# Seven products instead of eight in more of the gate and up columns, and a norm's sum two steps later

## The chip, the cores and the metric

The kernel is one program on one core of a Trainium2 chip. TensorE (PE in the profile) does the matrix products, VectorE (DVE) and ScalarE (ACT) the elementwise work, GpSimd (POOL) a little of it, and SyncE (SP) issues most of the DMAs. The metric is the device time of one execution in microseconds (us), the median of several runs.

## The reference

One layer on 256 rows of width 2048, in float32:

```python
x = x + 0.5 * swiglu(rms_norm(x, ffn1_norm), w_gate, w_up, w_down)     # FFN 1
u, q, k, v = split(rms_norm(x, mix_norm) @ w_in)
y_ssm = glu(s5(u))                                                      # state-space heads
y_sb = stick_breaking_attention(rms_norm(q), rms_norm(k), v)
x = x + concat(rms_norm(y_ssm), rms_norm(y_sb)) @ w_out
x = x + 0.5 * swiglu(rms_norm(x, ffn2_norm), w_gate, w_up, w_down)      # FFN 2
x = x + rms_norm((p @ w_ple_proj) * sigmoid(rms_norm(x, ple_norm) @ w_ple_gate))

def swiglu(h, w_gate, w_up, w_down):
    return (silu(h @ w_gate) * (h @ w_up)) @ w_down
```

The gate and up weights are 2048 x 5632, the down weights 5632 x 2048. All weights of the two FFNs are read once.

## The kernel before

**The float32 product.** Each float32 operand is split into a high part (a cast, on ScalarE) and a low part (what the cast left, a subtraction on VectorE). A product is then three matmuls of 128x128 by 128x512: high by high (L305), low activation by high weight (L306), high activation by low weight (L310). Weights arrive in a `raw` tile of four k tiles (128 rows of k each) by 512 columns, 1 MB, in a ring of five. `split` (L178) makes of each half of it, two k tiles, a tile `whi` (L181) and a tile `wlo` (L184), in rings of four. The 256 rows are two row tiles, so a half costs 2 x 2 x 3 = 12 matmuls. After each half `step()` advances the generators that run beside (transposes, norms, and in FFN 1 the preparation of the state-space part). `put_off(n, f)` runs `f` after `n` such steps.

**Gate and up.** Each FFN has 11 blocks of 512 columns, f = 0 to 10. A plain block runs all k (16 k tiles, eight halves) for the gate and then for the up columns: 16 halves. In FFN 1 (i=1, `bg` is the preparation) all blocks are plain. In FFN 2 block 0 is plain, and blocks 1 to 10 use the class `Seven`.

**Seven.** For a quarter of k, gate and up together, two row tiles and two halves of k make 2x2 by 2x2 blocks, so eight products of six matmuls each. `chunk(kb)` does quarter kb with seven products instead (Winograd's form of Strassen's method): 42 matmuls instead of 48. Three of the products use weights as they are. Four use sums of weights: VectorE adds them (`add`, L487, ring `sum` of two), ScalarE casts the sum to `shi`, and VectorE subtracts for `slo` (rings of three). These are called own products below, with their low parts `slo`. Against them stand `sum_forms` of the activations, made once per quarter of k from `whole_rows` (L426) with four additions (L441) and a split. `column(side, kbs)` does the quarters that are left over in the plain way, side 0 the gate and side 1 the up columns. The banks are combined afterwards: `opened` adds products 1, 6 and 7 (L574 to L576), `gated` products 2, 4 and 5 (L580 to L583), and L593 and L595 finish the block. Before, a block of FFN 2 is one chunk (quarter 0), then three quarters of the gate, then three of the up columns. The down projections of both FFNs use `Seven` too, by plans of their own.

**Order.** A scheduler chooses the order of the instructions on each engine within the data's dependences and the rings. Only pinned instructions keep their written place. Each engine then runs its own list in order.

**The norm in the middle.** `glu` writes the state-space output; its squares are added up on GpSimd (`add_square`, L1304 on ScalarE and L1305 on GpSimd), and `rms(steps, ...)` sums them over rows with two small matmuls against ones (L1289, pinned), `steps` steps later, and takes the inverse root (`rsqrt_mean`, L198 to L209, with a table load before ScalarE's square root at L203). The first user of the result is L1438, which takes the output projection's banks to x.

Of the kernel before, what the change touches and what calls it, by code (L numbers as in the profile page):

```python
# [33 lines left out]
def layer_kernel(ctx: ExitStack, tc: tile.TileContext, a: dict, shapes: dict, out: bass.AP):  # L34
# [3 lines left out]
    SW = shapes["ssm_d"][1]  # L38
# [34 lines left out]
    def phase(name):  # L73
        return tc.tile_pool(name=name, bufs=1, reuse_waits="tile")
# [354 lines left out]
        )  # L429
        return u.rearrange("p j n -> p (j n)").rearrange("p (j x b) -> p j x b", j=4, b=32)  # L430

    def sum_forms(pool, u):

        sums = pool.tile([P, 2, NB], F32, tag="sum", name=uid("rows"), bufs=2)
        s = sums.rearrange("p j n -> p (j n)").rearrange("p (z j x b) -> p z j x b", z=4, j=2, b=32)
        (a11, a21), (a12, a22) = ([u[:, k : k + 2, 4 * t : 4 * t + 4] for t in range(TT)] for k in (0, 2))
        for z, (x, y, op) in enumerate((
            (a21, a22, ALU.subtract), (s[:, 0], a11, ALU.subtract),
            (a11, a21, ALU.subtract), (a12, s[:, 1], ALU.add),
        )):  # L440
            nc.vector.tensor_tensor(out=s[:, z], in0=x, in1=y, op=op)  # L441
        both = halves("n")
        split(*both, sums.rearrange("p j n -> p (j n)").rearrange("p (z t) -> p z t", z=4))
        return both

# [93 lines left out]
    def ffn(i, xn, nxt, bg=None):  # L539
        wg, wu, wd = (a[f"ffn{i}_w_{s}"][0] for s in ("gate", "up", "down"))  # L540
        hT = []
        pools = ExitStack()
        early = 8 if bg else NF
        sevens = None if bg else pools.enter_context(phase(f"sums{i}"))
        hp = pools.enter_context(phase(f"h{i}"))
        side = ExitStack()
# [14 lines left out]
                hT.append(by_tile(hf, n_pair))  # L561

        for f in range(NF):
            if prep and f == min(early, NF - 1):
                finish(prep)
                side.close()
                prep = None
                hp = pools.enter_context(phase(f"h{i}b"))
            if sevens and f:
                sg, hh = com("sg"), com("h")  # L570
                gate_cols, up_cols = ([u[:, t * NB : (t + 1) * NB] for t in range(TT)] for u in (sg, hh))

                def opened(s, g=gate_cols, u=up_cols):
                    nc.scalar.copy(g[0], s.bank(1))  # L574
                    nc.vector.tensor_tensor(out=u[0], in0=s.bank(6), in1=g[0], op=ALU.add)
                    nc.vector.tensor_tensor(out=u[1], in0=s.bank(7), in1=u[0], op=ALU.add)  # L576

                def gated(s, g=gate_cols, u=up_cols, hh=hh):
                    for z, (ps, other) in enumerate(((s.bank(2), g[0]), (s.bank(4), u[1]))):
                        nc.vector.tensor_tensor(out=g[z], in0=ps, in1=other, op=ALU.add)  # L580
                        nc.scalar.activation(g[z], g[z], AF.Silu, scale=xn.rs(z))
                    v = hh.rearrange("p (t n) -> p t n", t=TT)
                    nc.vector.tensor_tensor(  # L583
                        out=v, in0=s.bank(5).unsqueeze(1).to_broadcast([P, TT, NB]), in1=v, op=ALU.subtract
                    )

                s = Seven(xn, lambda kb: sums[kb], ((wg, f * NB), (wu, f * NB)), sevens)
                s.chunk(0, shared)
                put_off(0, opened, s)
                s.column(0, (1, 2, 3), True)  # L590
                put_off(0, gated, s)
                s.column(1, (1, 2, 3), True)
                nc.vector.tensor_tensor(out=hh, in0=s.banks[3.8], in1=hh, op=ALU.add)  # L593
                for t in range(TT):
                    nc.vector.scalar_tensor_tensor(  # L595
                        out=up_cols[t], in0=up_cols[t], scalar=xn.rs(t), in1=gate_cols[t], op0=ALU.mult, op1=ALU.mult
                    )
                put_off(2, turned, hp, f, hh)
                continue

            def gate():
                for t in range(TT):
                    nc.scalar.activation(sg[:, t * NB : (t + 1) * NB], pg[t], AF.Silu, scale=xn.rs(t))

            first = ()
            if f == 0 and bg:
                warm_up(10)
                first = first_quarters(wg, xn)
            if f == 0 and not bg:
                both = gemm_pair(xn, ((wg, 0), (wu, 0)), KD)  # L610
                pg = next(both)
                sums = [sum_forms(sevens, whole_rows(sevens, xn(0)))]
            else:
                pg = gemm_block(xn, wg, f * NB, KD, first)
            sg = com("sg")
            if f == 0 and bg:
                for n in range(ND):
                    put_off(n, load_x, n)
                    put_off(n + 2, xn.squares, n)
                put_off(6, gate)  # L620
            else:
                gate()
            pu = gemm_block(xn, wu, f * NB, KD) if f or bg else next(both)
            if prep and f == 0:
                start(prep)
            hh = com("h")
            for t in range(TT):
                nc.vector.scalar_tensor_tensor(
                    out=hh[:, t * NB : (t + 1) * NB], in0=pu[t], scalar=xn.rs(t),
                    in1=sg[:, t * NB : (t + 1) * NB], op0=ALU.mult, op1=ALU.mult,  # L630
                )
            put_off(2, turned, hp, f, hh)
# [6 lines left out]
        def act(k):  # L639
            hi, lo = halves("h")  # L640
            split(in_32(hi), in_32(lo), rows(k))
            return hi, lo

        if not sevens:
            sevens = pools.enter_context(phase(f"sums{i}"))

        def gather(x, ps, scale):
            nc.vector.scalar_tensor_tensor(out=x, in0=ps, scalar=scale, in1=x, op0=ALU.mult, op1=ALU.add)
# [692 lines left out]
    def glu(pool, zs):  # L1341

        w = a["ssm_w_glu"][0]
        sq_acc = get(pool, "sqg", T)
        parts = []
        for n in range(SW // NB):
            ps = [acc(), acc()]
            for k0 in range(0, SW // P, 4):
                zhi, zlo = zs[k0 // 4]
                for h, hi, lo in weight_halves(w, k0, 4, n * NB):  # L1350
                    for part in range(2):
                        for j in range(2):
                            kt = k0 + 2 * h + j
                            for c in range(4):
                                o = ps[c // 2][:, (c % 2) * T : (c % 2 + 1) * T]
                                cs = slice(c * P, (c + 1) * P)
                                zj = 2 * h + j
                                if part == 0:
                                    nc.tensor.matmul(
                                        o, lhsT=hi[:, j, cs], rhs=zhi[:, zj, :], start=kt == 0 and c % 2 == 0,  # L1360
                                        stop=False, skip_group_check=True,
                                    )
                                    nc.tensor.matmul(
                                        o, lhsT=hi[:, j, cs], rhs=zlo[:, zj, :], start=False, stop=False,
                                        skip_group_check=True,
                                    )
                                else:
                                    nc.tensor.matmul(
                                        o, lhsT=lo[:, j, cs], rhs=zhi[:, zj, :], start=False,
                                        stop=kt == SW // P - 1, skip_group_check=True,  # L1370
                                    )
                    step()
            sg, y = com("sg"), com("h")
            hi, lo = halves("n")
            for c in range(4):
                nc.scalar.activation(
                    sg[:, c * T : (c + 1) * T], ps[c // 2][:, (c % 2) * T : (c % 2 + 1) * T], AF.Sigmoid,
                    bias=col("ssm_b_glu", 4 * n + c),
                )
            for t in range(TT):  # L1380

                su = sg.rearrange("p (c s t k) -> p c s t k", c=4, s=SL, t=TT)[:, :, :, t, :]
                zu = zt[0][:, :, 4 * n : 4 * n + 4, t * NC // TT : (t + 1) * NC // TT].rearrange("p s c k -> p c s k")
                yu = y.rearrange("p (c t s k) -> p c s t k", c=4, s=SL, t=TT)[:, :, :, t, :]
                nc.vector.tensor_tensor(out=yu, in0=su, in1=zu, op=ALU.mult)
            split_each(
                hi, lo, y.rearrange("p (c t) -> p c t", t=T), [col("out_norm_ssm", 4 * n + c) for c in range(4)]
            )
            for c in range(4):
                add_square(pool, sq_acc, y[:, c * T : (c + 1) * T], 4 * n + c == 0)  # L1390
            parts.append((hi, lo))
        return parts, rms(3, sq_acc, SW)


    n1, nm, n2, npl = Normed("ffn1_norm", load_turned), Normed("mix_norm"), Normed("ffn2_norm", kinds="hhnn", late=0), Normed("ple_norm", late=0)
# [256 lines left out]
```

## Time and profile before

| | |
|---|---|
| median of 3 runs | 1859.77 us (1859.67 to 1860.08) |
| the profiled execution | 1859.97 us, its span 1858.1 us |
| PE, PEld, DVE, ACT, POOL busy | 1848.8, 1530.4, 1350.9, 991.8, 62.8 us |
| matmuls recorded | 9098 |
| granted TensorE clock | 1.00 |

A row of the timeline or of the groups names the line, the engine, the operation, the tile written and the tiles read; "idle before" is the time in which the engine stood still before it, with what it then waited for. PEld is the load of weights into TensorE, which runs beside the matmuls.

### The profile page before, as it was taken

How to read it: one execution, taken by the hardware profiler on the slowest of the kernel's cores; microseconds unless marked ns; L12 is line 12 of the kernel's file. 1: busy time of each engine (PE TensorE's matmuls, PEld its weight loads, DVE VectorE, ACT ScalarE, POOL GpSimd, SP SyncE). 2: the span in 40 equal slices, each digit the busy share in tenths (PEclk: the TensorE clock that was granted, in tenths of full speed). 3: DMA queues.
4: the chain of work that ended last, by engine and by line, in shares of the span. 5: the costliest groups of instructions: out<-in, count | busy, mean ns of one | idle time of the engine just before them, and what ended most of it. 6: DMA issues, size and time to landing. Idle time of an engine off the chain costs nothing.

```text
span 1858.1 us, 23916 instructions
## 1 busy us (share of the span) xinstructions
PE 1848.8 (100%) x9098; PEld 1530.4 (82%) x9098; DVE 1350.9 (73%) x1599; ACT 991.8 (53%) x1147; POOL 62.8 (3%) x108
## 2 busy tenths in 40 slices
PE   9999999999999999999999999999999999999998
PEld 7888888888888888888888888888888888888887
DVE  8967764555688976687567677878788868897755
ACT  7444444444455656456695555555554545565654
POOL 0011000000000000010021000000000000000000
PEclk9999999999999999999999999999999999999999
DMA  9888868676656667675646776576666675666663
GB/s 330 283 278 269 256 218 231 201 230 200 217 188 219 200 208 255 183 260 166 218 153 201 236 266 216 192 226 204 221 210 206 195 244 183 212 198 225 200 226 125
DMA packets 232307, 406.37 MB, mean 219 GB/s; under 512 B 26784, under 2 KB 50720, under 8 KB 231904
## 3 DMA queue, kind: packets, MB, share of 16 engines
q1 hardware_dynamic: 227824, 392.81, 64.6%
q0 software_dynamic: 3648, 10.62, 1.8%
q8 instruction: 71, 1.16, 0.3%
q10 hardware_dynamic: 720, 1.41, 0.2%
q14 instruction: 44, 0.36, 0.1%
HBM read 373.46 MB, written 11.93 MB: 207 GB/s over the span
## 4 chain that ended last, share of the span: by engine, by line
PE 96%; ACT 2%; DVE 1%; DMA 0%; POOL 0%; issue 0%; SPq 0%; DVEq 0%; POOLq 0%
PE acc L305 22%; PE acc L310 22%; PE acc L306 22%; PE aux L306 7%; PE aux L305 7%; PE aux L310 7%; PE acc L480 2%; PE acc L481 2%; PE acc L483 2%; PE aux L480 1%; PE aux L481 1%; PE aux L483 1%; PE aux L1114 0%; ACT whi L181 0%; DMA raw<-in_ffn_w_gate 0%; ACT nhi L191 0%
## 5 line engine op out<-in xcount | busy, mean ns | idle before, releaser
L184 DVE TENSOR_TENSOR wlo<-raw,whi 128x1024 fp32r<-128x1024 f32 x650 | 789.0, 1223 | 412.3 <-ACT whi L181 398.7
L181 ACT CAST whi<-raw 128x1024 fp32r<-128x1024 f32 x650 | 680.9, 1053 | 761.6 <-PE acc L306 497.9
L305 PE MATMUL acc<-whi,nhi 128*128 128x512 f32 x1408 | 550.8, 391 | 1.3 <-ACT whi L273 0.8
L306 PE MATMUL acc<-whi,nlo 128*128 128x512 f32 x1408 | 548.3, 389 | 0.0
L310 PE MATMUL acc<-wlo,nhi 128*128 128x512 f32 x1408 | 384.4, 389 | 0.1
L305 PEld LDWEIGHTS acc<-whi,nhi 128*128 128x128 f32 x1408 | 264.3, 188 | 58.2 <-ACT whi L273 1.9
L310 PEld LDWEIGHTS acc<-wlo,nhi 128*128 128x128 f32 x1408 | 264.2, 188 | 55.6 <-DVE wlo L184 0.6
L306 PEld LDWEIGHTS acc<-whi,nlo 128*128 128x128 f32 x1408 | 264.3, 188 | 54.2 <-DVE nlo L274 0.3
L305 PE MATMUL acc<-whi,hhi 128*128 128x512 f32 x416 | 161.8, 389 | 0.0
L306 PE MATMUL acc<-whi,hlo 128*128 128x512 f32 x416 | 161.8, 389 | 0.0
L305 PE MATMUL aux<-whi,hhi 128*128 128x512 f32 x384 | 149.4, 389 | 0.0
L306 PE MATMUL aux<-whi,hlo 128*128 128x512 f32 x384 | 149.4, 389 | 0.0
L310 PE MATMUL acc<-wlo,hhi 128*128 128x512 f32 x416 | 126.7, 389 | 0.0
L310 PE MATMUL aux<-wlo,hhi 128*128 128x512 f32 x384 | 118.2, 389 | 0.0
L306 PEld LDWEIGHTS acc<-whi,hlo 128*128 128x128 f32 x416 | 78.1, 188 | 16.2
L305 PEld LDWEIGHTS acc<-whi,hhi 128*128 128x128 f32 x416 | 78.1, 188 | 16.2
L310 PEld LDWEIGHTS acc<-wlo,hhi 128*128 128x128 f32 x416 | 78.1, 188 | 16.2
L310 PEld LDWEIGHTS aux<-wlo,hhi 128*128 128x128 f32 x384 | 72.1, 188 | 15.0
L305 PEld LDWEIGHTS aux<-whi,hhi 128*128 128x128 f32 x384 | 72.1, 188 | 15.0
L306 PEld LDWEIGHTS aux<-whi,hlo 128*128 128x128 f32 x384 | 72.1, 188 | 15.0
L184 DVE TENSOR_TENSOR slo<-sum,shi 128x1024 fp32r<-128x1024 f32 x64 | 77.9, 1218 | 0.0
L181 ACT CAST shi<-sum 128x1024 fp32r<-128x1024 f32 x64 | 67.4, 1053 | 16.3 <-DVE sum L487 13.2
(324 smaller groups left out, 1739.6 us busy)
## 6 DMA issues: line engine op xcount, KB each, us to landing
raw<-in_ffn_w_up SPq DMA_DIRECT2D x88, 1024.0 KB, 5.7
raw<-in_ffn_w_down SPq DMA_DIRECT2D x88, 1024.0 KB, 5.1
raw<-in_ffn_w_gate SPq DMA_DIRECT2D x86, 1024.0 KB, 5.8
raw<-in_w_in SPq DMA_DIRECT2D x32, 1024.0 KB, 5.8
raw<-in_w_out SPq DMA_DIRECT2D x16, 1024.0 KB, 5.3
raw<-in_w_ple_gate SPq DMA_DIRECT2D x16, 1024.0 KB, 5.5
hT<-mid SPq DMA_DIRECT2D x160, 64.0 KB, 2.7
h<-mid SPq DMA_DIRECT2D x176, 32.0 KB, 3.8
```

Of the source, the lines that this page charges most:

```text
L181: copy = nc.scalar.copy(hi, src)
L184: nc.vector.tensor_tensor(out=lo, in0=src, in1=hi.bitcast(F32), op=ALU.subtract)
L305: nc.tensor.matmul(ps[t], lhsT=lh, rhs=hi[:, j, cols], start=start and j == 0, stop=False)
L306: nc.tensor.matmul(ps[t], lhsT=ll, rhs=hi[:, j, cols], start=False, stop=False)
L310: nc.tensor.matmul(ps[t], lhsT=lh, rhs=lo[:, j, cols], start=False, stop=stop and j == 1)
L480: nc.tensor.matmul(ps, lhsT=lh[j], rhs=hi[:, j], start=begin and j == 0, stop=False)
L481: nc.tensor.matmul(ps, lhsT=ll[j], rhs=hi[:, j], start=False, stop=False)
L483: nc.tensor.matmul(ps, lhsT=lh[j], rhs=lo[:, j], start=False, stop=z in final and j == 1)
```

## The change

There are four edits.

1. FFN 2: every odd block (1, 3, 5, 7, 9) does two quarters of k as chunks: chunk 0, the gate's quarters 2 and 3, chunk 1, the up columns' quarters 2 and 3. The combining (`opened`, then `gated`) follows chunk 1. The sum forms of quarter 1 are made as well.
2. FFN 1: blocks 7 to 10 use `Seven`. Block 7 does the gate's quarters 1 to 3 first, then chunk 0, then the up columns' quarters 1 to 3. Blocks 8 and 10 have two chunks, block 9 has one.
3. For that, the sum forms of quarters 0 and 1 are made at block 7 of FFN 1, and the preparation that runs beside FFN 1 is finished there (`finish(prep)`) instead of at block 8.
4. The sum of squares of the state-space output is taken five steps later instead of three.

```diff
-        early = 8 if bg else NF
+        early = 7 if bg else 0
...
-            if prep and f == min(early, NF - 1):
+            if prep and f == early:
                 finish(prep)
                 side.close()
                 prep = None
+                sevens = pools.enter_context(phase(f"sums{i}"))
                 hp = pools.enter_context(phase(f"h{i}b"))
+                sums = [sum_forms(sevens, whole_rows(sevens, xn(kb)), "h") for kb in range(2)]
...
-                s.chunk(0, shared)
-                put_off(0, opened, s)
-                s.column(0, (1, 2, 3), True)
+                two = f % 2 == (0 if bg else 1)
+                if f == early:
+                    s.column(0, (1, 2, 3))
+                    s.chunk(0, (*shared, 2, 4))
+                    put_off(0, opened, s)
+                elif two:
+                    s.chunk(0)
+                    s.column(0, (2, 3))
+                    s.chunk(1, (*shared, 2, 4))
+                    put_off(0, opened, s)
+                else:
+                    s.chunk(0, shared)
+                    put_off(0, opened, s)
+                    s.column(0, (1, 2, 3), True)
                 put_off(0, gated, s)
-                s.column(1, (1, 2, 3), True)
+                s.column(1, (2, 3) if two and f != early else (1, 2, 3), True)
...
-                sums = [sum_forms(sevens, whole_rows(sevens, xn(0)))]
+                sums = [sum_forms(sevens, whole_rows(sevens, xn(kb))) for kb in range(2)]
...
-        return parts, rms(3, sq_acc, SW)
+        return parts, rms(5, sq_acc, SW)
```

The new lines shift the numbers: L574 to L583 become L576 to L585, L593 and L595 become L606 and L608, L628 becomes L641, and L979 and everything behind it is ten higher (L1304 is L1314, for example). L184, L441 and L487 stay.

The first place is VectorE at block 7 of FFN 1. Before, these rows are the low parts of plain halves only (in a plain block there are 16 of them):

```order
L184 TENSOR_TENSOR wlo_2912<-raw_2909,whi_2911 128x1024
L184 TENSOR_TENSOR wlo_2916<-raw_2909,whi_2915 128x1024
L184 TENSOR_TENSOR wlo_2951<-raw_2948,whi_2950 128x1024
L184 TENSOR_TENSOR wlo_2955<-raw_2948,whi_2954 128x1024
L184 TENSOR_TENSOR wlo_2989<-raw_2986,whi_2988 128x1024
```

In the changed kernel the second sum form (`rows`, `hlo`) and the chunk's sums and own low parts stand between them:

```order
L441 TENSOR_TENSOR rows_2832<-whole_2830,rows_2832 128x256
L184 TENSOR_TENSOR wlo_2955<-raw_2950,whi_2954 128x1024
L487 TENSOR_TENSOR sum_2965<-raw_2950,raw_2952 128x1024
L184 TENSOR_TENSOR hlo_2838<-rows_2832,hhi_2837 128x1024
L184 TENSOR_TENSOR wlo_3016<-raw_2950,whi_3015 128x1024
L184 TENSOR_TENSOR slo_2968<-sum_2965,shi_2967 128x1024
L487 TENSOR_TENSOR sum_2978<-sum_2965,raw_2952 128x1024
L184 TENSOR_TENSOR wlo_3026<-raw_2952,whi_3025 128x1024
L487 TENSOR_TENSOR sum_2991<-sum_2978,raw_2950 128x1024
L184 TENSOR_TENSOR slo_2981<-sum_2978,shi_2980 128x1024
L184 TENSOR_TENSOR wlo_3039<-raw_3036,whi_3038 128x1024
L184 TENSOR_TENSOR slo_2994<-sum_2991,shi_2993 128x1024
```

Between two plain low parts there are now additions and the low parts of sums, and wlo_3039, of the up columns, comes ahead of the chunk's last low parts.

The second place is VectorE in FFN 2 where the next chunk's sums begin. Before, the first sums (L487) come late in a single block, among plain low parts:

```order
L184 TENSOR_TENSOR wlo_9999<-raw_9992,whi_9998 128x1024
L487 TENSOR_TENSOR sum_10119<-raw_10104,raw_10106 128x1024
L487 TENSOR_TENSOR sum_10132<-sum_10119,raw_10106 128x1024
L580 TENSOR_TENSOR sg_9794<-acc_9866,sg_9794 128x512
L184 TENSOR_TENSOR wlo_10034<-raw_10031,whi_10033 128x1024
L580 TENSOR_TENSOR sg_9794<-acc_9843,h_9795 128x512
L184 TENSOR_TENSOR slo_10122<-sum_10119,shi_10121 128x1024
L583 TENSOR_TENSOR h_9795<-acc_9817,h_9795 128x1024
```

In the changed kernel, at the end of a double block, they come right behind the last own low part of that block's chunk 1 (slo_10175), with all of the combining behind them:

```order
L184 TENSOR_TENSOR slo_10175<-sum_10172,shi_10174 128x1024
L487 TENSOR_TENSOR sum_10300<-raw_10285,raw_10287 128x1024
L487 TENSOR_TENSOR sum_10313<-sum_10300,raw_10287 128x1024
L577 TENSOR_TENSOR h_9962<-aux_9997,sg_9961 128x512
L184 TENSOR_TENSOR slo_10303<-sum_10300,shi_10302 128x1024
L578 TENSOR_TENSOR h_9962<-aux_9997,h_9962 128x512
L582 TENSOR_TENSOR sg_9961<-acc_10033,sg_9961 128x512
L582 TENSOR_TENSOR sg_9961<-acc_10010,h_9962 128x512
L184 TENSOR_TENSOR wlo_10249<-raw_10246,whi_10248 128x1024
L585 TENSOR_TENSOR h_9962<-acc_9984,h_9962 128x1024
```

The five combining steps that a block had spread over its columns stand together at the boundary of two chunks.

The third place is ScalarE around the norm's square root. Before, the table load and the root (L203) stand ahead of the last four squares (L1304), which come some rows later:

```order
L181 COPY whi_8207<-raw_8201 128x1024
L203 ACT_TABLE_LOAD
L203 ACTIVATE sm_8146<-sm_8144 128x2
L181 COPY whi_8263<-raw_8261 128x1024
L191 ACTIVATE nhi_8223<-aux_8178,gains 128x256 x4
L181 COPY whi_8267<-raw_8261 128x1024
```

In the changed kernel the four squares (now L1314) come first:

```order
L191 ACTIVATE nhi_8365<-aux_8305,gains 128x256 x4
L181 COPY whi_8409<-raw_8403 128x1024
L1314 ACTIVATE sqp_8375<-aux_8305 128x256
L1314 ACTIVATE sqp_8378<-aux_8305 128x256
L1314 ACTIVATE sqp_8381<-aux_8305 128x256
L1314 ACTIVATE sqp_8384<-aux_8305 128x256
L203 ACT_TABLE_LOAD
L203 ACTIVATE sm_8333<-sm_8331 128x2
```

The root, and with it L1448 (L1438 before), now stands behind the four squares. On PE the two pinned matmuls (L1289, now L1299) move behind two more halves and the attention output's small matmuls.

On SP the rest of the preparation's DMAs (eight writes of scr_h, eight reads m, one write of scr_m) was spread among six loads of weights. In the changed kernel only two loads stand among them.

More of the change, by code (lines that the diff above doesn't have):

```diff
@@ L430, in whole_rows, with sum_forms @@
         return u.rearrange("p j n -> p (j n)").rearrange("p (j x b) -> p j x b", j=4, b=32)
-    def sum_forms(pool, u):
+    def sum_forms(pool, u, kind="n"):
         sums = pool.tile([P, 2, NB], F32, tag="sum", name=uid("rows"), bufs=2)
@@ L441, in sum_forms @@
             nc.vector.tensor_tensor(out=s[:, z], in0=x, in1=y, op=op)
-        both = halves("n")
+        both = halves(kind)
         split(*both, sums.rearrange("p j n -> p (j n)").rearrange("p (z t) -> p z t", z=4))
@@ L642, in act @@
             return hi, lo
-        if not sevens:
-            sevens = pools.enter_context(phase(f"sums{i}"))
         def gather(x, ps, scale):
```

## The prediction

> **What bounds the kernel now.** I read the page first: busy times, then the chain of work that ended last.
>
> ```profile
> PE 1848.8 (100%) x9098; PEld 1530.4 (82%) x9098; DVE 1350.9 (73%) x1599; ACT 991.8 (53%) x1147; POOL 62.8 (3%) x108
> PEclk9999999999999999999999999999999999999999
> PE 96%; ACT 2%; DVE 1%; DMA 0%; POOL 0%; issue 0%; SPq 0%; DVEq 0%; POOLq 0%
> ```
>
> TensorE is busy for 1848.8 of the span's 1858.1 us at the full granted clock, and the chain is TensorE's for 96%. VectorE is at 73% on average. What does TensorE wait for? The waits of PE:
>
> ```profile
> PE aux L1289 <- POOL sqg L1305: 1.8, 1, 1.8
> PE aux L248 <- POOL ones L125: 1.1, 1, 1.1
> PE acc L305 <- ACT whi L273: 0.8, 1, 0.8
> PE acc L305 <- ACT whi L181: 0.4, 1, 0.4
> ```
>
> That is 4.1 us in all, 1.8 of it at the norm that edit 4 touches. So a matmul less is its time less, as long as the other engines keep up. Averages don't tell that, so I took the busy times of the engines over single blocks: one plain block of FFN 1 (about block 8), and two neighbours in FFN 2, each with one chunk. The columns are PE, PEld, DVE, ACT and POOL busy (with counts), the clock, the DMA share and GB/s.
>
> ```profile
> 359.60:403.10 43.50, 43.50 (x194) 36.02 (x193) 23.06 (x21) 18.03 (x19) 0.00 (x0) 1.00 0.69 216
> 1134.00:1176.30 42.30, 42.30 (x188) 34.93 (x187) 33.10 (x32) 21.57 (x23) 0.00 (x0) 1.00 0.70 222
> 1176.30:1218.60 42.30, 42.30 (x188) 34.93 (x187) 35.22 (x35) 21.66 (x23) 0.00 (x0) 1.00 0.62 201
> ```
>
> A chunk brings TensorE from 43.5 to 42.3 us and VectorE from 23.1 to some 34.2 us (the mean of the two), with the combining in it. TensorE waits for nothing in either.
>
> **What a chunk saves.** The timeline of PE, the first matmul of a chunk (L480), and the first behind it (L305):
>
> ```profile
> 1176.49 0.39 PE L480 MATMUL acc<-whi,hhi 128*128 128x512 f32 x1
> ...
> 1186.13 0.39 PE L305 MATMUL acc<-whi,hhi 128*128 128x512 f32 x1
> ```
>
> The chunk's 42 matmuls take 1186.13 − 1176.49 = 9.64 us, 0.2295 each. A plain block of 16 halves, 192 matmuls, in 43.5 us gives 0.2266 each. The quarter pair that a chunk replaces has 48, so 10.88 us. Saved: 1.24 us a chunk, and the two windows agree (43.5 − 42.3 = 1.2). The change adds five chunks in FFN 2 and six in FFN 1 (1 + 2 + 1 + 2), 66 matmuls less: 11 × 1.24 = **13.6 us**. Casts cost nothing: ScalarE is busy for half of each window, and a double block adds it three more casts.
>
> **What it adds on VectorE.** Four sums and three low parts a chunk. Their price is not their duration but the distance of their starts, which the timeline of DVE shows ahead of a chunk:
>
> ```profile
> 1166.16 1.22 DVE L487 TENSOR_TENSOR sum<-sum,raw 128x1024 f32<-128x1024 f32 x1
> 1167.31 1.22 DVE L184 TENSOR_TENSOR wlo<-raw,whi 128x1024 fp32r<-128x1024 f32 x1
> 1168.44 1.22 DVE L184 TENSOR_TENSOR slo<-sum,shi 128x1024 fp32r<-128x1024 f32 x1
> 1169.58 1.22 DVE L184 TENSOR_TENSOR wlo<-raw,whi 128x1024 fp32r<-128x1024 f32 x1
> ...
> 1181.12 1.22 DVE L184 TENSOR_TENSOR slo<-sum,shi 128x1024 fp32r<-128x1024 f32 x1
> ...
> 1189.73 1.23 DVE L184 TENSOR_TENSOR wlo<-raw,whi 128x1024 fp32r<-128x1024 f32 x1 [1.48 <-ACT whi L181]
> ```
>
> Starts are 1.13 to 1.15 apart, 1.135 on average, although each lasts 1.22. So a second chunk costs 7 × 1.135 = 7.9 us, and a double block needs 34.2 + 7.9 = 42.1 us of VectorE against 43.5 − 2 × 1.24 = 41.0 of TensorE. Alone it would be too much, but in FFN 2 a single block follows: 76.3 against 83.3 us a pair. The slack is there as gaps of 1.48 us between the column's low parts (last row).
>
> The Trainium skill speaks against this price: its page "VectorE: DVE Perf Modes", section "The DRAIN you can't avoid", says that the next operation does not start until the pipe has emptied. With a full 1.22 us for each of the some 32 large operations of a double block, it would need 2.7 us more, 44.8 against 41.0; the rows above, 1.135 apart, do not show such a hold, and the section itself adds that an operation that is not held starts earlier.
>
> **FFN 2's boundaries.** The last own low part of the chunk above starts at 1181.12 and is done at 1182.34. TensorE wants it behind five products, near 1182.7: a margin of 0.4 us, here at the end of a single block. At a double block's end the combining (two additions of 0.68 and 0.69, two of 0.69, one of 1.22) stands at the same place:
>
> ```profile
> 1184.58 0.68 DVE L575 TENSOR_TENSOR h<-aux,sg 128x512 f32<-128x512 f32 x1
> 1185.29 0.69 DVE L576 TENSOR_TENSOR h<-aux,h 128x512 f32<-128x512 f32 x1
> L580 DVE TENSOR_TENSOR sg<-acc,h 128x512 f32<-128x512 f32 x10 | 6.9, 688 | 1.3 <-PE acc L310 1.3
> L583 DVE TENSOR_TENSOR h<-acc,h 128x1024 f32<-128x1024 f32 x10 | 12.2, 1218 | 0.0
> ```
>
> Counting the changed order off from the end of chunk 1 at these distances, VectorE runs without a gap to the next chunk's last low part, and comes just in time: 0 to 0.5 us each. There are four such boundaries to a next chunk and one to the down projection. I take **0.8 us** in all, from 0 (the margin) to 5 (1 us each, one operation too many). Chunk 1 inside a double block has some 5 us of lead.
>
> **FFN 1, blocks 7 to 10.** Here VectorE gets six chunks in four blocks, and two sum forms of an addition (1.135), four quarter additions and a low part (1.135). The quarter rows:
>
> ```profile
> L441 DVE TENSOR_TENSOR rows<-hT 128x256 f32<-128x256 f32 x12 | 4.5, 419 | 0.0
> ...
> 316.41 1.41 DVE L628 SCALAR_TENSOR_TENSOR h<-acc,sm,sg 128x512 f32<-128x512 f32 x2 [1.09 <-PE acc L310]
> ...
> 318.87 1.30 DVE L216 STREAM_TRANSPOSE mid<-h 128x512 f32<-128x512 f32 x2
> ```
>
> At some 0.36 apart (an estimate between the 0.42 they last and the overlap seen above) that is 3.7 a form, 7.4 for both. The sum is 2 × 34.2 + 2 × 42.1 + 7.4 = 160.0 us of VectorE in 4 × 43.5 − 6 × 1.24 = 166.6 of TensorE, 96% full. Such a stretch can't be free of waits, since the work comes in heaps. In block 7 the changed order has, from L628 at 316.41 to the chunk's last own low part, 22 large operations (25.0 us), eight quarter rows (2.9) and L628 and L216 (2.7): ready at 347.0. TensorE begins block 7 at 316.15 and reaches that low part behind 131 matmuls (29.7), at 345.85: 1.2 us late. The same count gives 1.3 at block 8's first chunk, next to nothing at its second, 1.3 at block 9's. I take **4.0 us**; from 1 (the scheduler's interleaving of column halves covers it) to 8 (each chunk late by 1.3).
>
> **The norm.** TensorE's wait of 1.77 us at L1289 goes, since GpSimd is done two halves earlier than it is asked:
>
> ```profile
> 968.53 0.71 PE L1289 MATMUL aux<-ones,sqg 128*128 128x128 f32 x4 [1.77 <-POOL sqg L1305]
> 963.57 4.91 POOL L1305 TENSOR_TENSOR sqg<-sqg,sqp 128x256 f32<-128x256 f32 x4 [11.90 <-ACT sqp L1304]
> 969.13 1.28 ACT L203 ACT_TABLE_LOAD   x1
> 971.84 0.59 PE L1313 MATMUL aux<-w,v 128*128 128x256 f32 x2
> ...
> 974.23 0.38 PE L1317 MATMUL aux<-w,v 128*128 128x128 f32 x2
> 977.44 1.40 DVE L1438 SCALAR_TENSOR_TENSOR x<-acc,sm,x 128x512 f32<-128x512 f32 x2
> 982.22 0.38 ACT L1304 ACTIVATE sqp<-aux 128x256 f32<-128x256 f32 x1 [1.34 <-POOL sqa L1305]
> ```
>
> What is late next: the root stands behind four squares, two of which wait for GpSimd's additions of about 1.2 us each. TensorE would come to the two matmuls at 968.53 − 1.77 = 966.76, plus 5.44 for two halves and 2.7 for the attention's small matmuls (971.84 to 974.6), which now stand ahead of them: 974.9. Counted on from there, the squares end near 978.6, the table load near 979.9, and L1448 hands back its banks near 982 and 982.6, while TensorE is through its pair of columns near 980.8. It waits some 1.3 us there for a bank. Gain 1.77 − 1.3, about **0.4 us**, between +1.8 (no such wait) and −1.5 (the squares' second half late by one addition for each of them).
>
> **The sum.** Against the profiled 1859.97 us (1858.1 of span, 1.87 around it; 0.20 above the median): 13.6 + 0.4 − 4.0 − 0.8 = 9.2 us less. From the median, 1859.8 − 9.2 = **1850.6 us**.
>
> **Rivals.** A: no wait at all is left, the matmul count decides alone: 1859.8 − 13.6 − 0.4 = 1845.8. For it: before, 10 chunks of FFN 2 run without a wait. Against: there VectorE has gaps ahead of every chunk, and 4% slack is far less.
>
> B, slower: VectorE falls behind for good in blocks 7 to 10. A chunk's own product is a chain of sum (1.22), ScalarE's cast and subtraction (1.22), and a row gives the cast:
>
> ```profile
> L181 ACT CAST whi<-raw 128x1024 fp32r<-128x1024 f32 x650 | 680.9, 1053 | 761.6 <-PE acc L306 497.9
> ```
>
> So 1.22 + 1.05 + 1.22 = 3.5 us. If each of the six chunks bares one such chain, 21 us go: 1859.8 − 13.6 − 0.4 + 21 + 0.8 = 1867.6. It decides from 14.0 us of waits on, 1.27 for each added chunk. For it: 96%. Against: three slots for own parts let the chains overlap. Were the 114 large operations of these blocks 1.22 apart and not 1.135, VectorE would need 9.7 us more, 169.7 against 166.6. That is what the Trainium skill's rule weighed above would make of them.
>
> C: the drained preparation blocks SP. Before, its DMAs were spread out:
>
> ```profile
> 291.29 2.49 SPq L979 DMA_DIRECT2D scr_h<-hq  x4
> ...
> 307.73 2.18 SPq L986 DMA_DIRECT2D m<-scr_h  x4
> ...
> 324.06 0.37 SPq L990 DMA_DIRECT2D scr_m<-m  x1
> scr_h<-hq SPq DMA_DIRECT2D x8, 32.0 KB, 5.1
> m<-scr_h SPq DMA_DIRECT2D x2, 128.0 KB, 6.4
> ```
>
> In one go, eight writes (2 × 2.49), a landing (5.1), eight reads (2 × 2.18) and their landing (6.4) are 21 us, with one load of weights let through; TensorE eats one every 5.44 us (half a quarter pair), and five slots hold 27 us. It fits by a few us. If not, loads for block 7 are late by about one landing more, 5 us: 1855.7.
>
> **Chances.** Forecast 0.65, A 0.15, B 0.12, C 0.08. The range has to leave out no more than 0.2: from A, 1845.5, up to 1857.0, where FFN 1 loses 8, the boundaries 3 and the norm gains nothing (2.6 us gained). A measurement can tell 0.2%, 3.7 us, from no change: below 1856.1 is faster. Faster: nearly all of the forecast, A, half of C, 0.81. Within: the rest of these and a corner of B, 0.09. Slower: 0.10, B.
>
> **What would show it.** PE's busy time down by 13 to 14 us and L305's groups with fewer matmuls; new waits of PE for `slo` or `whi` (L184, L181) between 330 and 470 us, a few of about 1 us each; blocks 8 and 10 of FFN 1 near 41 to 43 us; double blocks of FFN 2 near 41.0 and the singles behind them 42.3 to 42.8; the row PE aux L1289 gone, and one wait of 1 to 1.5 us for L1448 near 980. I am wrong if the waits in FFN 1 pass 8 us, if a wait at every boundary of FFN 2 passes 1 us, or if DMA stands as the releaser of block 7's casts.

## The result, and the profile after

The changed kernel takes 1851.99 us (1851.55 to 1852.70, five runs), the kernel before 1859.88 (1859.67 to 1860.13): 7.9 us less, a ratio of 0.9958 [0.9944, 0.9973]. The forecast was 1850.6 us, 9.2 less.

The busy times and the chain on the page of the changed kernel:

```profile
span 1850.6 us, 23946 instructions
PE 1838.3 (99%) x9032; PEld 1518.5 (82%) x9032; DVE 1460.6 (79%) x1718; ACT 1027.4 (56%) x1187; POOL 63.3 (3%) x108
PEclk9999999999999999999999999999999999999999
PE 92%; DVE 3%; DMA 2%; ACT 2%; SPq 1%; issue 1%; DVEq 0%; ACTq 0%
```

The 66 matmuls are gone (9098 to 9032), VectorE has 110 us more to do, and the chain is no longer TensorE's alone. What TensorE waits for, in the waits of PE:

```profile
PE acc L480 <- ACT shi L181: 2.6, 2, 1.7
PE acc L305 <- ACT whi L181: 1.7, 3, 1.1
PE aux L248 <- POOL ones L125: 1.1, 1, 1.1
PE aux L480 <- ACT shi L181: 0.9, 1, 0.9
PE acc L310 <- DVE wlo L184: 0.3, 2, 0.2
```

The first and fourth rows are new: L480 is a chunk's matmul, `shi` the cast of a sum. So is the 1.1 us in the second row, which stands at the norm; the section on why the prediction was right comes back to it. The wait for GpSimd at the norm is gone. Where the time went is read from the same matmul in both timelines of PE: the first of FFN 1's down projection, of FFN 2's gate, of FFN 2's down projection, and the last. Before:

```profile
490.51 0.39 PE L305 MATMUL acc<-whi,hhi 128*128 128x512 f32 x1
1048.41 0.39 PE L305 MATMUL acc<-whi,hhi 128*128 128x512 f32 x1
1514.73 0.39 PE L305 MATMUL acc<-whi,hhi 128*128 128x512 f32 x1
1852.05 1.12 PE L1557 MATMUL aux<-e,diag 128*128 128x512 f32 x2
```

And after:

```profile
487.58 0.39 PE L305 MATMUL acc<-whi,hhi 128*128 128x512 f32 x1
1046.39 0.39 PE L305 MATMUL acc<-whi,hhi 128*128 128x512 f32 x1
1506.75 0.39 PE L305 MATMUL acc<-whi,hhi 128*128 128x512 f32 x1
1844.05 1.12 PE L1567 MATMUL aux<-e,diag 128*128 128x512 f32 x2
```

The differences are −2.93, −2.02, −7.98 and −8.00. So FFN 1's gate and up gained 2.9 us (0.1 of it at the start of the program), the middle gave back 0.9, FFN 2's gate and up gained 6.0, and behind it nothing changed. The span is 7.5 shorter; the last half microsecond lies behind the last matmul.

The busy times by stretch, for blocks 7 to 10 of FFN 1 in one piece, and then for a single, a double and again a single block of FFN 2:

```profile
316.20:487.60 171.40, 167.88 (x735) 137.23 (x734) 162.85 (x165) 95.73 (x100) 4.40 (x8) 1.00 0.64 213
1134.00:1176.00 42.00, 42.00 (x187) 34.67 (x186) 33.96 (x34) 21.38 (x23) 0.00 (x0) 1.00 0.72 227
1176.00:1217.00 41.00, 41.00 (x181) 33.76 (x180) 40.97 (x40) 24.27 (x26) 0.00 (x0) 1.00 0.60 203
1217.00:1259.00 42.00, 42.00 (x186) 34.69 (x185) 34.07 (x34) 21.29 (x22) 0.00 (x0) 1.00 0.71 226
```

In FFN 1 VectorE is busy for 162.9 us while TensorE computes for 167.9, and TensorE stands still for 3.5. In FFN 2 VectorE is busy for 40.97 of the double block's 41.0 us, and TensorE waits for nothing.

### The profile page after: what moved, and what is told of

Its sections match the earlier page's. It is cut to its first block, busy times and chain, and to the rows that moved or that the text cites. A ratio compares the mean times of both kernels' runs of the same rounds, so it can differ in the third digit from the quotient of the medians.

```text
span 1850.6 us, 23946 instructions
## 1 busy us (share of the span) xinstructions
PE 1838.3 (99%) x9032; PEld 1518.5 (82%) x9032; DVE 1460.6 (79%) x1718; ACT 1027.4 (56%) x1187; POOL 63.3 (3%) x108
## 4 chain that ended last, share of the span: by engine, by line
PE 92%; DVE 3%; DMA 2%; ACT 2%; SPq 1%; issue 1%; DVEq 0%; ACTq 0%
PE acc L305 18%; PE acc L310 18%; PE acc L306 18%; PE aux L305 7%; PE aux L306 7%; PE aux L310 7%; PE acc L480 3%; PE acc L481 2%; PE acc L483 2%; PE aux L480 2%; PE aux L483 2%; PE aux L481 2%; DVE wlo L184 1%; SPq L1170 1%; DMA raw<-in_w_in 1%
## 5 line engine op out<-in xcount | busy, mean ns | idle before, releaser
L184 DVE TENSOR_TENSOR wlo<-raw,whi 128x1024 fp32r<-128x1024 f32 x639 | 772.0, 1221 | 297.9 <-ACT whi L181 295.1
L305 PE MATMUL acc<-whi,nhi 128*128 128x512 f32 x1232 | 482.9, 392 | 1.8 <-ACT whi L181 1.7
L306 PE MATMUL acc<-whi,nlo 128*128 128x512 f32 x1232 | 479.9, 390 | 0.0
L310 PE MATMUL acc<-wlo,nhi 128*128 128x512 f32 x1232 | 340.6, 389 | 0.2 <-DVE wlo L184 0.2
L305 PEld LDWEIGHTS acc<-whi,nhi 128*128 128x128 f32 x1232 | 231.5, 188 | 52.2 <-ACT whi L181 3.0
L310 PEld LDWEIGHTS acc<-wlo,nhi 128*128 128x128 f32 x1232 | 231.2, 188 | 48.8 <-DVE wlo L184 0.6
L306 PEld LDWEIGHTS acc<-whi,nlo 128*128 128x128 f32 x1232 | 231.6, 188 | 47.2
L305 PE MATMUL acc<-whi,hhi 128*128 128x512 f32 x376 | 146.3, 389 | 0.0
L181 ACT CAST shi<-sum 128x1024 fp32r<-128x1024 f32 x108 | 113.4, 1052 | 43.1 <-DVE sum L487 39.6
L305 PE MATMUL aux<-whi,hhi 128*128 128x512 f32 x344 | 133.8, 389 | 0.0
L184 DVE TENSOR_TENSOR slo<-sum,shi 128x1024 fp32r<-128x1024 f32 x108 | 130.9, 1216 | 0.6 <-ACT shi L181 0.5
L310 PE MATMUL acc<-wlo,hhi 128*128 128x512 f32 x376 | 114.6, 389 | 0.2 <-DVE wlo L184 0.2
L310 PE MATMUL aux<-wlo,hhi 128*128 128x512 f32 x344 | 106.0, 389 | 0.0
L306 PE MATMUL aux<-whi,nlo 128*128 128x512 f32 x240 | 93.4, 389 | 0.0
L305 PE MATMUL aux<-whi,nhi 128*128 128x512 f32 x240 | 93.4, 389 | 0.0
L310 PEld LDWEIGHTS acc<-wlo,hhi 128*128 128x128 f32 x376 | 70.5, 188 | 15.2 <-DVE wlo L184 0.6
L305 PEld LDWEIGHTS acc<-whi,hhi 128*128 128x128 f32 x376 | 70.6, 188 | 14.6
```

The costliest lines, as they stand in the source:

```text
L181: copy = nc.scalar.copy(hi, src)
L184: nc.vector.tensor_tensor(out=lo, in0=src, in1=hi.bitcast(F32), op=ALU.subtract)
L305: nc.tensor.matmul(ps[t], lhsT=lh, rhs=hi[:, j, cols], start=start and j == 0, stop=False)
L306: nc.tensor.matmul(ps[t], lhsT=ll, rhs=hi[:, j, cols], start=False, stop=False)
L310: nc.tensor.matmul(ps[t], lhsT=lh, rhs=lo[:, j, cols], start=False, stop=stop and j == 1)
```

## The experiments

**The parts alone.** Three kernels have one part of the change each: the double blocks of FFN 2, the chunks of FFN 1, the later sum of squares.

```diff
 # FFN 2 alone: the kernel before, with the branches of the change, its second sum form in FFN 2, and
+                two = f % 2 == 1
...
 # FFN 1 alone: the changed kernel, with
-                two = f % 2 == (0 if bg else 1)
+                two = bool(bg) and f % 2 == 0
...
-                sums = [sum_forms(sevens, whole_rows(sevens, xn(kb))) for kb in range(2)]
+                sums = [sum_forms(sevens, whole_rows(sevens, xn(0)))]
...
-        return parts, rms(5, sq_acc, SW)
+        return parts, rms(3, sq_acc, SW)
...
 # the norm alone: the kernel before, with
-        return parts, rms(3, sq_acc, SW)
+        return parts, rms(5, sq_acc, SW)
```

> The kernel before with the double blocks of FFN 2 alone. Theory: VectorE comes just in time at the boundaries, so five chunks save 5 x 1.24 = 6.2 us less some 0.3 us of waits: about 1854.0 us, and PE shows no wait over 0.5 us in the gate and up blocks of FFN 2. Rival: every boundary of a double block costs 1 us or more: 1855 to 1857 us, with five waits of PE to be seen. Second rival: a part of the whole change's gain in FFN 2 comes from the other edits: over 1857 us.

> The changed kernel with the edits of FFN 1 alone (FFN 2 as before, the norm's sum after three steps). Theory: six chunks save 7.4 us, three to four chunks wait about 1 to 1.7 us for a cast of a sum that VectorE made late, so blocks 7 to 10 end 2.9 us earlier. If the 1.2 us that the changed kernel loses later, in FFN 1's down projection, belongs to these edits, the time is about 1858.2 us; if it was chance there, about 1857.0 us. Rival: the edits of FFN 1 cost more than they save: over 1859.9 us.

> The kernel before with the norm's sum after five steps instead of three. Theory: the wait of 1.8 us for GpSimd goes, one of 1.1 us comes at the next pair of banks, and the small matmuls follow each other as before: 0.5 us less, 1859.4 us. Rival: nothing is left of it or it costs: 1859.9 us or more.

Measured on one chip, with 1860.13 us before: FFN 2 alone 1855.34 (0.9975 [0.9966, 0.9984]), FFN 1 alone 1859.20 (0.9994 [0.9986, 1.0003]) and the norm alone 1860.12 (0.9999 [0.9990, 1.0008]). FFN 2 alone shows no wait in its gate and up blocks, which take 5.9 us less than before in its trace, as in the whole change. So FFN 2 carries most of the gain. Its time of 1855.34 lies where the first rival's would, but the five waits of that rival aren't there; what is missing to 1854.0 lies outside these blocks. FFN 1 alone gains 0.9, less than its measurement can tell from nothing, and less than either figure expected. In its trace blocks 7 to 10 gain 2.8 us again, with the same three waits; 1.0 us goes before FFN 2, and 0.8 in FFN 2's own down projection, where a cast waits 2.0 us for a load of weights (1.1 before). The norm alone moves nothing measurable, where 0.5 us was expected; in the traces the place itself gains 0.5 to 0.6 us (below). The three gains add to 5.7 us of the 7.1 to 7.9 that the whole change gave in two sittings. What differs lies in the down projections and at the program's start; I did not settle it further. Edit 3, the earlier end of the preparation, was never run without the chunks, so the two are not told apart.

**What an operation costs VectorE.** Two chunks in every block of FFN 2 make VectorE the bound there.

```diff
-                two = f % 2 == (0 if bg else 1)
+                two = f % 2 == 0 if bg else True
```

> The changed kernel with two chunks in every block from 1 to 10 of FFN 2, five chunks more. TensorE's work alone would be 6.2 us less (1845.8 us). Theory: VectorE then bounds these blocks, at 42.1 us each (operations 1.135 us apart) against TensorE's 41.0, so ten blocks take 421 us where five pairs took 416.6: about 1856.5 us, with waits of PE for VectorE in nearly every block. Rival (operations held to their full 1.22 us): 44.8 us a block, 448 us: about 1883 us. Rival (VectorE has more room than counted): no waits, 1846 us.

1854.46 us (0.9970 [0.9959, 0.9982]). Six of these blocks (4 to 9), cut where the first chunk of each begins:

```profile
1213.00:1254.20 41.20, 41.20 (x181) 33.68 (x180) 40.53 (x40) 24.16 (x26) 0.00 (x0) 1.00 0.72 230
1254.20:1296.50 42.30, 41.37 (x181) 33.66 (x180) 41.93 (x41) 24.69 (x26) 0.00 (x0) 1.00 0.59 199
1296.50:1339.50 43.00, 41.38 (x181) 33.67 (x180) 42.39 (x41) 24.25 (x26) 0.00 (x0) 1.00 0.68 220
1339.50:1382.50 43.00, 41.38 (x181) 33.72 (x180) 42.37 (x42) 23.88 (x26) 0.00 (x0) 1.00 0.58 195
1382.50:1423.90 41.40, 41.40 (x182) 33.61 (x181) 40.01 (x40) 24.34 (x26) 0.00 (x0) 1.00 0.72 229
1423.90:1466.90 43.00, 41.38 (x182) 33.65 (x181) 42.42 (x41) 24.03 (x26) 0.00 (x0) 1.00 0.58 196
sum 253.90, PE 248.10 PEld 201.99 DVE 249.65 ACT 145.35 POOL 0.00; mean PE 41.35 PEld 33.66 DVE 41.61 ACT 24.23 POOL 0.00
```

VectorE is busy for 41.61 us a block, where the prediction's count gave 42.1, and for 249.65 of these 253.9 us: it has next to no slack. TensorE waits instead, 0.93 us at 1260.36 and 1.62 us each at 1303.82, 1346.83 and 1431.15. That is four of the ten blocks, not nearly all of them as expected. The rule in the Trainium skill's page "VectorE: DVE Perf Modes" (section "The DRAIN you can't avoid"), read as no overlap at all, would give 44.8 us a block; these operations overlap, and the measurement decides. Against the changed kernel five chunks more cost 2.5 us by its first runs (1851.99), 1.4 by its repeat below (1853.09), and 1.7 in this stage by the traces; 4.5 was expected. The first chunks of the first three blocks still start 41.0 us apart; only then is the lead used up.

**Amount or place.** The first experiment here repeats the changed kernel. The second takes the second chunks of FFN 1 away, so that VectorE has less to do. The third leaves the amount and moves the chunk of each single block behind the gate's quarters.

```diff
 # one chunk a block in FFN 1
-                two = f % 2 == (0 if bg else 1)
+                two = not bg and f % 2 == 1
...
 # column first
-                    s.chunk(0, shared)
+                    s.column(0, (1, 2, 3))
+                    s.chunk(0, (*shared, 2, 4))
                     put_off(0, opened, s)
-                    s.column(0, (1, 2, 3), True)
```

> The changed kernel once more, beside the next two on the same chip. Theory: blocks 7 to 10 of FFN 1 end 2.8 us earlier than before, the gate and up blocks of FFN 2 take 6.0 us less, the norm 0.5, and the 1.2 us lost at the end of FFN 1's down projection come from weight loads that landed late behind a queue of transposes there, which differs from run to run: 7 to 9 us less than before, and the loss there anything from 0 to 1.2 us. Rival: that loss belongs to the change and comes again in full.

> The changed kernel with one chunk instead of two in blocks 8 and 10 of FFN 1 (four added chunks there, not six). Theory: VectorE's heap decides; it has 7.9 us less to do in each of those blocks, so the waits at the chunks of blocks 8 and 9 (0.97 and 1.67 us) go or shrink and only block 7's 0.9 stays: 4 x 1.24 - 0.9 = 4.1 us less in blocks 7 to 10 against 2.8 with six chunks, so 1 us faster than the changed kernel. Rival: the waits come from where a chunk stands, not from how much is done, and stay; then two chunks less cost 2.5 us.

> The changed kernel with the gate's three quarters ahead of the chunk in every block with one chunk (as block 7 of FFN 1 has it), so that 16.3 us of plain columns lie between the end of a block with two chunks and the next chunk. Theory: VectorE then has time to make the sums, and the 1.67 us at block 9 of FFN 1 go; FFN 2 had no waits and stays, unless the later combining delays the next block: 1 to 2 us faster than the changed kernel. Rival: block 10 then waits in its place (its first chunk comes 16.3 us behind block 9's instead of 32.6): no gain.

Beside 1860.22 us before: 1853.09 again (0.9959 [0.9945, 0.9973]), 1853.43 with less work (0.9963 [0.9949, 0.9977]), and 1849.91 with the other place (0.9946 [0.9933, 0.9959]). With less work the wait at block 8 stayed at 0.97 us and block 7's grew to 1.7; only block 9's went. So the expectation of 1 us failed: blocks 7 to 10 gain 1.6 us in that trace, against 2.7 in the repeat. Less work in block 8 did end the wait at block 9 behind it, but the two chunks given up for that are worth more. The other place ends the same wait and gives nothing up: 3.2 us less than the repeat, where 1 to 2 were expected; 2.0 of them are in blocks 7 to 10 by the traces, the rest is not settled. In the timeline of PE for the changed kernel, the three waits of blocks 7, 8 and 9:

```profile
337.80 0.50 PE L480 MATMUL aux<-shi,hhi 128*128 128x512 f32 x1 [0.89 <-ACT shi L181]
366.04 0.50 PE L480 MATMUL acc<-shi,nhi 128*128 128x512 f32 x1 [0.97 <-ACT shi L181]
409.56 0.50 PE L480 MATMUL acc<-shi,nhi 128*128 128x512 f32 x1 [1.67 <-ACT shi L181]
```

And with the column first, where the last row above has no successor, and block 10 does not wait in its place:

```profile
338.30 0.50 PE L480 MATMUL aux<-shi,hhi 128*128 128x512 f32 x1 [0.89 <-ACT shi L181]
366.55 0.50 PE L480 MATMUL acc<-shi,nhi 128*128 128x512 f32 x1 [0.97 <-ACT shi L181]
```

Why a chunk right at the start of a block is late is to be seen on ScalarE and VectorE of the changed kernel at block 8, ahead of the wait at 366.04. ScalarE:

```profile
364.94 1.04 ACT L181 CAST shi<-sum 128x1024 fp32r<-128x1024 f32 x1 [2.88 <-DVE sum L487]
```

VectorE:

```profile
361.23 1.21 DVE L184 TENSOR_TENSOR slo<-sum,shi 128x1024 fp32r<-128x1024 f32 x1
362.36 1.41 DVE L608 SCALAR_TENSOR_TENSOR h<-h,sm,sg 128x512 f32<-128x512 f32 x2
363.69 1.22 DVE L487 TENSOR_TENSOR sum<-sum,raw 128x1024 f32<-128x1024 f32 x1
364.82 0.70 DVE L216 STREAM_TRANSPOSE mid<-h 128x512 f32<-128x512 f32 x1
```

The cast waits 2.88 us for the third sum (363.69), and that stands behind the finishing of block 7 (L608). The heap consists of the chunk's own operations and the end of the block before it. A wait costs TensorE more than its idle time: two matmuls ahead of the last wait, from 407.28 to 409.56, take 2.28 us where two take 0.45, so 1.83 for an idle 1.67, and the first matmul behind it takes another 0.1 more than usual. Counted by such starts, the three waits take some 4.4 us, not 3.5.

**Taking the last waits away.** Three more kernels stand on the one with the column first: the second sum form made later; block 8's first chunk behind two gate quarters; and block 7's chunk also behind one quarter of the up columns. That kernel itself ran again beside the first two.

```diff
 # second form later
-                sums = [sum_forms(sevens, whole_rows(sevens, xn(kb)), "h") for kb in range(2)]
+                sums = [sum_forms(sevens, whole_rows(sevens, xn(0)), "h")]
...
+                    put_off(2, lambda: sums.append(sum_forms(sevens, whole_rows(sevens, xn(1)), "h")))
...
 # block 8, column first
-                    s.chunk(0)
-                    s.column(0, (2, 3))
+                    if bg and f == early + 1:
+                        s.column(0, (2, 3))
+                        s.chunk(0)
+                        s.column(1, (2,))
+                    else:
+                        s.chunk(0)
+                        s.column(0, (2, 3))
                     s.chunk(1, (*shared, 2, 4))
...
 # and block 7 later
                     s.column(0, (1, 2, 3))
+                    s.column(1, (1,))
                     s.chunk(0, (*shared, 2, 4))
...
```

> The kernel with the gate's quarters ahead of every single chunk, and in FFN 1 the sum form of quarter 1 (needed only in block 8) made two halves into block 7's up columns instead of ahead of its chunk. Theory: the forms are a part of VectorE's heap in block 7; 3.7 us less ahead of its chunk end the wait of 0.89 us there, but the same work then stands ahead of block 8's first chunk, whose 0.97 us stay or grow: 0 to 0.9 us faster than without the move. Rival: the waits at blocks 7 and 8 have nothing to do with the forms: both stay.

> The kernel with the gate's quarters ahead of every single chunk, and block 8 of FFN 1 in the order gate quarters 2 and 3, chunk 0, up quarter 2, chunk 1, up quarter 3. Theory: block 8's first chunk comes 10.9 us later, and its wait of 0.97 us goes, but only 5.4 us of plain columns lie between its two chunks instead of 10.9, so VectorE is late at the second by the 7 operations' 7.9 us less what it gained: the wait moves there, 0.5 to 1.5 us. About even. Rival: the wait at block 8 goes for good: 1 us faster.

> The kernel with the gate's quarters ahead of every single chunk once more, for the other two: about 1850 us, waits of 0.9 and 1.0 us at the chunks of blocks 7 and 8. The loss at the end of FFN 1's down projection was between 0.2 and 1.4 us in the six kernels with chunks in FFN 1 and nothing in the others; if it is these edits', it is over 0.1 us here again.

> The kernel with the gate's quarters first in single blocks and in block 8 of FFN 1, and in block 7 also one quarter of the up columns ahead of the chunk. Theory: VectorE is late at block 7's chunk because the sum forms and the chunk's sums stand in one heap; 5.4 us more of plain columns ahead of it end that wait of 0.9 us too, if the heap does not only move to block 8: 1 us faster than with block 8 alone, about 1847.6 us. Rival: block 8's first chunk, now 5.4 us closer, waits instead: no gain.

The form moved later costs 4 us: 1853.31 against 1849.29 for the same kernel without the move. As forecast, block 7's wait went; but the size at block 8 was far off. There the same work now stands in a fuller heap, and these three rows of PE's waits are all at its first chunk:

```profile
PE aux L480 <- ACT shi L181: 2.8, 1, 2.8
PE acc L483 <- DVE slo L184: 0.3, 1, 0.3
PE acc L480 <- ACT shi L181: 0.3, 1, 0.3
```

The waits are not the whole loss. Behind the wait of 2.81 us, which ends at 365.99, the granted clock is 0.60 for a while, and TensorE starts 10 matmuls where 15 are usual:

```profile
366.00:369.50 3.50, 3.50 (x10) 2.74 (x11) 3.50 (x5) 1.05 (x1) 0.00 (x0) 0.60 0.49 122
```

In the same kernel without the move, the stretch as long behind its wait of 0.97 us has 15 matmuls at a clock of 1.00. Nine matmuls from 366.56 on take 3.65 us instead of some 2.04, so 1.6 us are lost on top of the wait. No other wait for a chunk in these traces is longer than 1.7 us, and none of those shows it.

The two moves of chunks work: 1848.59 (0.9936 [0.9922, 0.9949]) with block 8's, 1847.63 (0.9932 [0.9919, 0.9944]) with both. These times lie too near each other, and to 1849.29, to tell the steps apart; the traces do: blocks 7 to 10 end 4.8 us earlier than before with the column first, 6.2 with block 8's move, and 7.2 with both. So my expectation that the wait would only move to block 8's second chunk was wrong. Of the waits for `shi`, the first leaves one:

```profile
PE aux L480 <- ACT shi L181: 0.9, 1, 0.9
```

The second leaves none, and this is its whole list:

```profile
PE acc L305 <- ACT whi L181: 1.5, 2, 1.1
PE aux L248 <- POOL ones L125: 1.1, 1, 1.1
PE acc L310 <- DVE wlo L184: 0.2, 1, 0.2
```

The same chunks, the same matmuls and the same operations on VectorE, in another order, take 4.4 us less than the changed kernel's first five runs (1847.63 against 1851.99; with the second five, 1853.09, it is 5.5).

**More chunks.** With that order the two-chunk blocks of FFN 2 can stand closer. Against the kernel with block 8's move:

```diff
-                two = f % 2 == (0 if bg else 1)
+                two = f % 2 == 0 if bg else f % 3 != 0
...
-                    if bg and f == early + 1:
+                    if not bg or f == early + 1:
...
```

> The same kernel without that last step, but FFN 2 with two chunks in blocks 1, 2, 4, 5, 7, 8 and 10 (two chunks more in all), in the order gate quarters 2 and 3, chunk 0, up quarter 2, chunk 1, up quarter 3. Theory: VectorE needs 2 x 42.1 + 34.2 = 118.4 us in 124.4 of TensorE, as full as FFN 1's blocks, and the order lets it keep up: 2 x 1.24 = 2.5 us saved, some waits of up to 1 us: 1846.5 to 1848.6 us. Rival: the two chunks of a block are now only 5.4 us apart, and VectorE, which can hold no more than three sums ahead, is late at the second in every such block by 1 us or more: 1853 us or above.

1847.23 us (0.9931 [0.9917, 0.9944]), beside 1859.97 before and 1847.63 for the kernel above, which differs by block 7's step. In FFN 2 one wait for `slo` of 0.7 us is left, at 1228.18. It is the fastest of the kernels by its median, though 0.4 us below the one above says nothing; by the traces its gate and up blocks of FFN 2 take 1.1 us less than with block 8's move alone, where 2.5 was forecast. The rival falls: with 5.4 us between a block's chunks VectorE keeps up.

## Why the prediction was right

**The gross gain** of 13.6 us stands: 66 matmuls less, and the FFN 2 stage, where nothing waits, gave 6.0 of its 6.2. (One slip of the sum: the range's upper end, from 2.6 us gained, is 1857.2 and not 1857.0.)

**FFN 1's waits** were forecast at 4.0 us, with 1.2, 1.3, nothing and 1.3 at the chunks. They are 0.89, 0.97, none and 1.67, 3.5 in all, and 4.4 counted by starts. The blocks and the cause are as counted, VectorE's queue without a gap (160.0 us counted, 162.9 measured); the place in the chunk is not. The prediction has TensorE late at the chunk's last own low part, in block 7 ready at 347.0. That low part is done at 346.90, and TensorE takes it at 347.36 without a wait: it had waited 10 us earlier, at 337.80, for the cast of the second sum, and blocks 8 and 9 wait for the cast of their third. Net of the waits blocks 7 to 10 gave 2.8 us, not 7.4 − 4.0 = 3.4. Rival A falls by these rows, and B as well: VectorE doesn't fall behind for good, it is late where a chunk follows a heap, and the moves of the chunks show that.

**FFN 2's boundaries** were taken at 0.8 us and cost 0.3 or less: 6.0 us net, not 5.4. By luck this makes up for FFN 1's 0.6. The forecast of singles at 42.3 and doubles at 41.0 holds.

**The norm** was forecast at 0.4 us and gives 0.5: the matmul ahead of it runs 1.52 us earlier than before, the first of FFN 2 2.02. The wait of 1.77 went and one of 1.12 came, at 980.38, near 980 as said. The profile names ScalarE's cast of weights as its releaser (row PE acc L305 <- ACT whi, 1.1), and for the second bank, 0.30 us long, L1448. PEld of the changed kernel:

```profile
980.35 0.19 PEld L305 LDWEIGHTS acc<-whi,nhi 128*128 128x128 f32 x1 [1.51 <-ACT whi L181]
980.95 0.19 PEld L305 LDWEIGHTS acc<-whi,nhi 128*128 128x128 f32 x1 [0.30 <-DVE x L1448]
```

ScalarE and VectorE there:

```profile
975.74 0.39 ACT L1314 ACTIVATE sqp<-aux 128x256 f32<-128x256 f32 x1 [1.11 <-POOL sqa L1315]
976.96 1.28 ACT L203 ACT_TABLE_LOAD   x1
978.37 1.98 ACT L181 CAST whi<-raw 128x1024 fp32r<-128x1024 f32 x2
973.90 1.22 DVE L184 TENSOR_TENSOR wlo<-raw,whi 128x1024 fp32r<-128x1024 f32 x1
979.49 2.73 DVE L1448 SCALAR_TENSOR_TENSOR x<-acc,sm,x 128x512 f32<-128x512 f32 x4
982.13 1.22 DVE L184 TENSOR_TENSOR wlo<-raw,whi 128x1024 fp32r<-128x1024 f32 x1
```

The cast can't be it. The half that starts at 980.38 begins its matmuls with the low part (L310) at 982.44, while VectorE's next low part, from 982.13, is not done before 983.35. So it uses the one of 973.90, and its high part was cast before that; the two casts from 978.37 on are for later halves. What does end just ahead of the two loads is L1448's first operation (at 980.24) and its second (at 980.90). So the step was right: squares, table load, root, then L1448 hands back its banks, 1.12 us late where the count gave 1.3.

**The missing 1.3 us** of the forecast's 9.2 were not in any of its terms. The lead of the changed kernel shrinks by 1.4 us between the first matmul of FFN 1's down projection and the norm, 1.2 of it inside that projection (235.64 us before, 236.82 after). It goes between 630 and 652 us, near the middle of the projection and not at its end, as the expectations above put it. There a load of weights lands late and ScalarE's cast waits for it. The cast, before and after:

```profile
633.85 2.00 ACT L181 CAST whi<-raw 128x1024 fp32r<-128x1024 f32 x2 [0.68 <-DMA raw<-in_ffn_w_down]
```

```profile
632.83 2.00 ACT L181 CAST whi<-raw 128x1024 fp32r<-128x1024 f32 x2 [1.86 <-DMA raw<-in_ffn_w_down]
```

In the repeated run that wait is 1.4 us and the loss 0.3. Over the traces the loss in the projection is 0.2 to 1.5 us in the eleven profiled runs with chunks in FFN 1 and none in the three without, so it seems to come with FFN 1's edits, in a size that differs from run to run. One step further back can be seen: ahead of that load SP issues 19 small DMAs of L229 (h<-mid, a part of a transpose), and these wait for an earlier load to land. SP's waits between 600 and 632 us, before and after:

```profile
SPq L229 <- DMA raw<-in_ffn_w_down: 0.6, 1, 0.6
```

```profile
SPq L229 <- DMA raw<-in_ffn_w_down: 1.8, 1, 1.8
```

This wait is 0.6 us in the three traces without a loss, 0.6 to 0.7 in the three that lose 0.2 to 0.3, and 0.9 to 2.1 in the other eight, which lose 0.3 to 1.5. That is agreement over 14 traces and no experiment. How the edits reach loads more than 100 us later is open. Rival C was another thing, the drained preparation ahead of block 7: no row of PE or VectorE waits there for a load.

## What to carry to other kernels

Trading matmuls for elementwise work pays as long as each stretch between two such trades has room for it on the other engine: compare the two engines' busy times by block, and price operations by the distance of their starts. At 95% fullness the place decides: put the piece that needs prepared operands behind plain work, not first in its block, where the end of the last block is in the same queue. Check a named releaser against the order of the tiles before you believe it: at the norm the profile named a cast that other matmuls were to use. Then look again at the whole trace, since a stage that isn't touched can give back a microsecond.

## What was not expected of the hardware

VectorE kept 1.135 us between starts of 1.22 us operations even where it was the bound (249.65 us busy in 253.9, 41.61 a block). Behind a wait of 2.81 us TensorE's granted clock was 0.60 for 3.5 us; behind the waits of 0.9 to 1.7 us its matmuls went on at their usual distance but for the first. And with a load that landed late in one stage, 0.2 to 1.5 us went between runs of kernels that differ more than 100 us earlier.
